# Delaying the first store of a DMA-streamed SiLU-multiply by one small DVE copy, so that it is not issued together with a load

## The chip, the cores, the metric

One core of one Trainium2 chip. The metric is the device time of one execution in microseconds (us), the median of a few runs. The profiler's span of one execution (from the program's first to its last instruction) is about 1.8 us shorter than that time, and is used only to compare spans with spans.

DVE is the vector engine, ACT the scalar engine, SP the sync engine, which only issues DMAs here. A load or a store is one DMA: an engine issues it into its queue, 16 DMA engines move it, and it lands when all of it has arrived. The trace records it in packets; a packet here is the piece that one DMA engine moves at a time, one contiguous run of one partition.

## The reference

```python
def setup_inputs():
    batch, seq, dim = (32, 512, 2048)
    return {'x': np.random.randn(batch, seq, dim).astype(np.float32)}

def reference(x):
    half_dim = x.shape[-1] // 2
    x1, x2 = x[..., :half_dim], x[..., half_dim:]          # (copies cut)
    silu_x1 = x1 * (1 / (1 + np.exp(-x1)))
    return (silu_x1 * x2).astype(np.float32)
```

134.22 MB are read and 67.11 MB written, with two light elementwise operations between them.

## The kernel before

The 16384 rows are cut into 16 tiles; a tile has 128 partitions with 8 rows each. Two input buffers (64 KB per partition each) and two output buffers (32 KB each) are used in turn. Loads are issued from ACT's queue, stores from SP's. After the multiplies of tile i, the store of tile i and the load of tile i+2 are both released by the same event, the last multiply.

```python
    K = 8
    KC = 2
    # ... (cut: tile plan, pools with bufs=2 each, views)
    def load(i):
        xt = in_pool.tile([P, K, in_cols], dt, name="xt")
        nc.scalar.dma_start(out=xt[:, :plan[i][1], :], in_=view(x_flat, i))
        loaded[i] = xt

    load(0)
    load(1)
    for i in range(n_tiles):
        # ... (cut)
        for c in range(0, k, KC):
            ce = min(c + KC, k)
            nc.scalar.activation(out=ot[:, c:ce, :], in_=xt[:, c:ce, :half], func=Silu)
            nc.vector.tensor_mul(out=ot[:, c:ce, :], in0=ot[:, c:ce, :], in1=xt[:, c:ce, half:])
            if last:
                nc.sync.dma_start(out=ov[:, c:ce, :], in_=ot[:, c:ce, :])
        if not last:
            nc.sync.dma_start(out=ov, in_=ot[:, :k, :])
        if i + 2 < n_tiles:
            load(i + 2)
```

## Time and profile before

| quantity | before | where it is read |
|---|---|---|
| time, median | 470.84 us (470.56 to 471.13, 3 runs) | the runs |
| span of the profiled run | 468.9 us | page |
| bytes moved, mean rate | 201.35 MB, 429 GB/s | page |
| DVE and ACT busy | 30%, 25% | page |
| DMA in a tile period of 29 us | share 1.00, 432 to 434 GB/s | table by windows |

The page of the kernel before, its lines on engines and DMA. A digit in the DMA line is the busy share of one fortieth of the span, in tenths; 9 means 90% or more.

```profile
span 468.9 us, 269 instructions
DVE 142.3 (30%) x64; ACT 118.2 (25%) x65; POOL 0.2 (0%) x4
DMA  9899999999999998999999999999999989999998
DMA packets 5042, 201.35 MB, mean 429 GB/s; under 512 B 560, under 2 KB 560, under 8 KB 560
```

No compute engine is busy for even a third of the time, while the DMA line stands at 8 or 9 in every slice. The table by windows of the same kernel says it more sharply. Its columns are the stretch, its length, each engine's busy time with the number of instructions, the clock, the share of the 16 DMA engines' time that was busy, and what they moved. (A share a little over 1 comes of counting each packet where it starts.)

```profile
core 0: us, DVE busy (x) ACT busy (x) POOL busy (x), PEclk, DMA share, GB/s
44.50:73.50 29.00, 8.89 (x4) 7.31 (x4) 0.00 (x0) 1.00 1.00 434
73.50:102.50 29.00, 8.90 (x4) 7.31 (x4) 0.00 (x0) 1.00 1.00 434
422.00:451.00 29.00, 8.89 (x4) 7.31 (x4) 0.00 (x0) 1.00 1.00 432
451.00:467.00 16.00, 8.90 (x4) 7.31 (x4) 0.00 (x0) 1.00 0.99 421
```

Even the end, from 451 us on, after the last load has landed, is full of stores. The timeline around the first store (start, duration, engine, line, operation; in brackets the idle time before and what ended it; an "x3" merges three issues into one line):

```profile
21.88 7.31 ACT L87 ACTIVATE ot<-xt 128x2048 f32<-128x2048 f32 x4 [19.31 <-DMA xt<-in_x_dram]
23.82 8.90 DVE L92 TENSOR_TENSOR ot<-ot,xt 128x2048 f32<-128x2048 f32 x4 [23.82 <-ACT ot L87]
32.74 51.99 SPq L100 DMA_DIRECT2D out_dram<-ot  x3
32.75 0.35 ACTq L74 DMA_DIRECT2D xt<-in_x_dram  x1
44.54 7.31 ACT L87 ACTIVATE ot<-xt 128x2048 f32<-128x2048 f32 x4 [15.36 <-DMA xt<-in_x_dram]
46.48 8.89 DVE L92 TENSOR_TENSOR ot<-ot,xt 128x2048 f32<-128x2048 f32 x4 [13.77 <-ACT ot L87]
55.41 0.37 ACTq L74 DMA_DIRECT2D xt<-in_x_dram  x1
73.53 7.31 ACT L87 ACTIVATE ot<-xt 128x2048 f32<-128x2048 f32 x4 [21.68 <-DMA xt<-in_x_dram]
```

The first store and load 2 are issued 5 ns apart. Load 1 lands at 44.5 us, 11.8 us after load 2 was issued; load 3 is issued at 55.4 us, and load 2 lands at 73.5. So the load queue always holds work. The chain of waits (start, duration, what) alternates between a load and 8.91 us of multiplies:

```profile
55.41 47.19 DMA xt<-in_x_dram
102.60 0.02 issue
102.62 1.92 ACT ot L87
104.54 0.02 issue
104.57 8.91 DVE ot L92 x4
113.47 0.02 issue
113.50 47.07 DMA xt<-in_x_dram
```

### The profile page before, as it was taken

To read this page: it belongs to the slowest core of one execution; us is meant where nothing else is said; L and a number is where in the kernel's file an instruction comes from. 1 tells how busy PE (TensorE), PEld (TensorE's weight loads), DVE (VectorE), ACT (ScalarE), POOL (GpSimd) and SP (SyncE) were. 2 spreads that over 40 slices of the span, in tenths; PEclk is the share of its full clock that TensorE was granted. 3 is DMA by queue.
4 is the path that set the end of the run, shared out by engine and by line. 5 is a ranking of instruction groups with operands and counts; after the bars stand their busy time and mean duration, and the time that the engine had idled before them with its cause. 6 is when DMAs were issued, how large, how long until landed. Compare 5 with 4: busy or idle time off the path is not lost.

```text
span 468.9 us, 269 instructions
## 1 busy us (share of the span) xinstructions
DVE 142.3 (30%) x64; ACT 118.2 (25%) x65; POOL 0.2 (0%) x4
## 2 busy tenths in 40 slices
DVE  0070705106061160601507025070250702407034
ACT  1142406023060330603206032060420604106051
POOL 0000000000000000000000000000000000000000
DMA  9899999999999998999999999999999989999998
GB/s 431 375 447 403 447 447 447 403 419 431 447 447 403 447 492 363 442 492 391 458 403 439 456 447 403 409 442 447 447 403 444 467 386 447 442 419 481 400 409 354
DMA packets 5042, 201.35 MB, mean 429 GB/s; under 512 B 560, under 2 KB 560, under 8 KB 560
## 3 DMA queue, kind: packets, MB, share of 16 engines
q10 hardware_dynamic: 2304, 134.22, 66.4%
q1 hardware_dynamic: 2736, 67.11, 33.2%
q14 instruction: 2, 0.02, 0.0%
HBM read 134.22 MB, written 67.11 MB: 429 GB/s over the span
## 4 chain that ended last, share of the span: by engine, by line
DMA 80%; DVE 15%; ACT 3%; DVEq 0%; issue 0%
DMA xt<-in_x_dram 80%; DVE ot L92 15%; ACT ot L87 3%; DVEq L128 0%
## 5 line engine op out<-in xcount | busy, mean ns | idle before, releaser
L92 DVE TENSOR_TENSOR ot<-ot,xt 128x2048 f32<-128x2048 f32 x64 | 142.3, 2286 | 319.5 <-ACT ot L87 319.5
L87 ACT ACTIVATE ot<-xt 128x2048 f32<-128x2048 f32 x64 | 116.9, 1897 | 338.8 <-DMA xt<-in_x_dram 338.8
L87 ACT ACT_TABLE_LOAD x1 | 1.3, 1283 | 1.3 <-PEq L117 1.3
L117 POOL MEMSET const-uint8-127<- 128x1 uint8 x1 | 0.1, 102 | 0.0
L117 POOL MEMSET const-bfloat16-1.0<- 128x1 bf16 x1 | 0.1, 101 | 0.0
L117 POOL MEMSET const-float32-0.0<- 128x1 f32 x1 | 0.1, 98 | 0.2 <-issue 0.2
L117 POOL MEMSET const-float32-1.0<- 128x1 f32 x1 | 0.1, 98 | 0.0
## 6 DMA issues: line engine op xcount, KB each, us to landing
out_dram<-ot SPq DMA_DIRECT2D x15, 4096.0 KB, 39.8
out_dram<-ot SPq DMA_DIRECT2D x4, 1024.0 KB, 5.7
xt<-in_x_dram ACTq DMA_DIRECT2D x16, 47.1
```

Source lines behind the costliest of these rows:

```text
L87: nc.scalar.activation(out=ot[:, c:ce, :], in_=xt[:, c:ce, :half], func=mybir.ActivationFunctionType.Silu,)
L92: nc.vector.tensor_mul(out=ot[:, c:ce, :], in0=ot[:, c:ce, :], in1=xt[:, c:ce, half:],)
L117: nc = _bacc.Bacc("TRN2", target_bir_lowering=False, num_devices=1)
```

## The change

The intent is that the first store should not be issued at the same moment as load 2. The store must wait for a copy that rewrites one row of its tile; the load waits for the multiplies only.

```diff
                 nc.sync.dma_start(out=ov[:, c:ce, :], in_=ot[:, c:ce, :])
+        if i == 0:
+            nc.vector.tensor_copy(out=ot[:, k - 1, :], in_=ot[:, k - 1, :])
         if not last:
             nc.sync.dma_start(out=ov, in_=ot[:, :k, :])
```

## The prediction

> **What bounds the kernel now.** The 16 DMA engines, all the time. The page gives 201.35 MB at a mean of 429 GB/s over a span of 468.9 us; DVE is busy 30%, ACT 25%. The table by windows shows a DMA share of 1.00 and 432 to 434 GB/s in every 29 us tile period. In the trace's packets a 64 KB load packet takes 2.42 us and a 32 KB store packet 1.21 us on an engine; all packets of an engine make about 465 us, of a window from 1.1 to 467 us. Load and store packets alternate, and no queue empties after the first store: each load is issued 11.8 us before the previous one lands (chain of waits, timeline), each store about 11 us before the previous one lands. DVE's 8.91 us per tile is on the drawn chain but hides behind those queued transfers. The Trainium skill ("DMA: Bandwidth & Descriptors", section "Issuing engines are not separate DMA queues") says that both issuing engines share the same 16 DMA engines and interleave; this trace agrees.
>
> **What the change does.** It removes nothing. It adds one DVE copy of 128x1024 f32, after tile 0 only. The multiply of 128x2048 takes 2.286 us, so at its rate the copy takes an estimated 1.2 us; the skill ("VectorE: DVE Perf Modes", section "Mode 2×_2P") gives f32 copies twice the rate, about 0.7 us. No instruction of this trace shows which. DVE idles 13.8 us there, so tile 1 isn't touched. The first store's issue moves from 32.75 us to about 33.5 us (34.0 at the slow rate). Load 2 stays at 32.75 us. Later pairs are still issued together.
>
> **How much lies on the critical path.** Almost nothing. Meanwhile the engines have load 1 (until about 43 us) and then load 2. The first store's packets, now at 38.9 us, stay or move by one load packet (2.42 us), and loads move ahead by the same work. The store of tile 0 lands at 66.2 us, 7.3 us before load 2 at 73.5 us, so its buffer is still free in time. At the end one more store packet may be queued behind the last load, so the tail stays full. Bytes and packet sizes are the same.
>
> The only loss that the change could remove: load packets that start at 35.7 us, just before the first store's, take 3.2 to 3.4 us in place of 2.42 on all 16 engines, 0.8 us lost once. Later pairs, also issued within 5 ns, show none, so I take it for the cost of the store queue's first use, which stays. If it came from the simultaneous issue it would go: 0.8 us (0.2%).
>
> **Prediction: 470.7 us, 469.4 to 472.0.** Faster by over 2%: 0.01; within 2%: 0.97; slower by over 2%: 0.02. A gain of 2% (9 us) is not there: only 2 to 4 us of the span are not moving packets.
>
> **What would show it.** A DVE copy of 0.6 to 1.2 us after tile 0's multiplies; the first store issued that much after load 2; the long packets near 35.7 us still there, or gone for 0.8 us; tile periods of 29.0 us, DMA share 1.00; the last load within 3 us of 451.0 us, the end within 1 us of 468.9.
>
> **What would make it wrong.** If the shifted order of packets lowered the rate in all tile periods: 0.6 us a tile would be 2%. If the later store made tile 2's activation wait for its buffer until the load queue ran empty, which needs a delay over 11 us. If load 2 waited for the copy, that would only cost hidden issue time.

## The result, and the profile after

| | before | after |
|---|---|---|
| time, median | 470.96 us (470.56 to 471.13, 4 runs) | 470.93 us (470.67 to 471.56, 4 runs) |
| ratio | | 1.0002, 95% interval 0.9985 to 1.002 |
| span of the profiled run | 468.9 us | 468.9 us |
| first store issued | 32.74 us | 33.53 us |
| its first packet | 38.88 us | 38.86 us |
| last load landed | 451.00 us | 451.03 us |

Ratios, here and below, are the mean time of one kernel's runs over that of the other's of the same rounds, so not quite the ratio of the medians quoted. Executions over 1.5% slower than the fastest of the same kernel are left out of the means.

The page of the kernel after:

```profile
span 468.9 us, 270 instructions
DVE 143.0 (31%) x65; ACT 118.2 (25%) x65; POOL 0.2 (0%) x4
DMA  9899999999999998999999999999999989999998
DMA packets 5042, 201.35 MB, mean 429 GB/s; under 512 B 560, under 2 KB 560, under 8 KB 560
L101 DVE COPY ot<-ot 128x1024 f32<-128x1024 f32 x1 | 0.7, 695 | 0.0
```

One instruction more, 0.695 us of DVE; the DMA line is the same digit for digit. The table by windows of the kernel after:

```profile
44.50:73.50 29.00, 8.90 (x4) 7.31 (x4) 0.00 (x0) 1.00 1.00 434
73.50:102.50 29.00, 8.90 (x4) 7.31 (x4) 0.00 (x0) 1.00 1.00 434
422.00:451.00 29.00, 8.89 (x4) 7.31 (x4) 0.00 (x0) 1.00 1.00 432
451.00:467.00 16.00, 8.90 (x4) 7.31 (x4) 0.00 (x0) 1.00 0.99 421
```

The timeline after, around the first store:

```profile
23.88 8.90 DVE L92 TENSOR_TENSOR ot<-ot,xt 128x2048 f32<-128x2048 f32 x4 [23.88 <-ACT ot L87]
32.81 0.33 ACTq L74 DMA_DIRECT2D xt<-in_x_dram  x1
32.81 0.69 DVE L101 COPY ot<-ot 128x1024 f32<-128x1024 f32 x1
33.53 51.22 SPq L103 DMA_DIRECT2D out_dram<-ot  x3
44.71 7.31 ACT L87 ACTIVATE ot<-xt 128x2048 f32<-128x2048 f32 x4 [15.47 <-DMA xt<-in_x_dram]
46.65 8.90 DVE L92 TENSOR_TENSOR ot<-ot,xt 128x2048 f32<-128x2048 f32 x4 [13.15 <-ACT ot L87]
```

The chain of waits after, the same stretch:

```profile
55.59 47.02 DMA xt<-in_x_dram
102.60 0.02 issue
102.63 1.92 ACT ot L87
104.55 0.02 issue
104.57 8.91 DVE ot L92 x4
113.48 0.02 issue
113.50 47.12 DMA xt<-in_x_dram
```

The load issued at 55.59 us in place of 55.41 lands at the same 102.60 us: what is issued later just waits less.

The change did to the issues just what it was meant to: the store now follows the load by 0.72 us. Nothing followed from it. On the DMA engines the first store packet starts when it did before, because those engines were busy with packets of load 1. On idle engines a store's first packet starts 0.9 us after its issue (delay27 below), so before about 33.6 us and after about 34.4 us. Each engine was then on a load packet that ran until about 35.7 us, and it took one more load packet before the store's. (Why one more, the records don't show; in delay4 and every_store_later it is up to two.) The copy used up 0.8 us of a wait that was 6.1 us long before (32.74 to 38.88) and 5.3 us long after (33.53 to 38.86). From there on the packets follow one another as before: the n-th load or store packet of the one trace starts within 0.25 us of that of the other, to the end. On an engine it reads as follows, L for a 64 KB load packet and S for a 32 KB store packet (my reading of the packet records, the first two tile periods):

```
before  L L L L L L L L L L L L L L L* S L S S L S L S L S L S L S L L S L S S L S L ...
after   L L L L L L L L L L L L L L L* S L S S L S L S L S L S L S L L S L S S L S L ...
        an L takes 2.418 us, an S 1.213 us; L* takes 3.2 to 3.4 us in both
```

All packets of one engine at these durations make 465.0 us; the window from the first packet to the last is 466.5 us. So about 1.5 us in the whole program are lost in packets that take too long: 0.6 us in the very first packets, and 0.8 to 0.9 us in L*, the last load packet before the first store packet. L* is the only thing that the change could have removed, and it is still there.

The Trainium skill ("DMA: Bandwidth & Descriptors", section "Queues, rings and completion order") says that each DMA engine takes turns between the queues that have work, a packet at a time. The trace agrees: L and S alternate, one to one, wherever both queues hold work. Since a load has 8 packets of 64 KB per engine and tile and a store 8 of 32 KB, one-to-one turns use up both at the same pace. The two places in a period where two S or two L follow each other are where the turn of the other queue goes to the four-byte record that signals a completion. The section "Where 436 GB/s comes from" puts the ceiling of the fabric at 435 GB/s; the trace shows 434 in a period. There is no room for a gain of even 2%.

### The profile page after: what moved, and what is told of

The parts are those of the page before. It is cut to its first block, busy times and chain, and to the rows that moved or that the text cites. A ratio compares the mean times of both kernels' runs of the same rounds, so it can differ in the third digit from the quotient of the medians.

```text
span 468.9 us, 270 instructions
## 1 busy us (share of the span) xinstructions
DVE 143.0 (31%) x65; ACT 118.2 (25%) x65; POOL 0.2 (0%) x4
## 4 chain that ended last, share of the span: by engine, by line
DMA 80%; DVE 15%; ACT 3%; DVEq 0%; issue 0%
DMA xt<-in_x_dram 80%; DVE ot L92 15%; ACT ot L87 3%; DVEq L131 0%
## 5 line engine op out<-in xcount | busy, mean ns | idle before, releaser
L92 DVE TENSOR_TENSOR ot<-ot,xt 128x2048 f32<-128x2048 f32 x64 | 142.3, 2286 | 318.8 <-ACT ot L87 318.8
```

## The experiments

Theory A: the DMA engines always have packets, so a delay of a DMA's issue costs or gains nothing as long as another queue holds work. Rival B: load 2 and the first store collide, which is what L* is, and a better separation would gain 0.8 us. Rival C: the separation gains something and the delay by the copy eats it. Part of my prediction was also that L* is the price of the store queue's first use; D, E and F below are its rivals. Twelve kernels ran. "Before" in each table is the kernel before, run on the same chip between them.

### A longer delay of the first store: 4.4, 26.7 and 40.1 us

```diff
         if i == 0:
-            nc.vector.tensor_copy(out=ot[:, k - 1, :], in_=ot[:, k - 1, :])
+            for _ in range(N):          # delay4: N = 1, delay27: N = 6, delay40: N = 9
+                nc.vector.tensor_copy(out=ot[:, :k, :], in_=ot[:, :k, :])
```

delay4:

> In place of one row, the whole of tile 0 is copied in place, so the first store is issued about 4.4 us after load 2[...]. Theory A (the DMA engines are never without packets, and the long load packets before the first store are the price of the store queue's first use): same time within 0.3%; the first store's packets come one or two load packets (2.42 or 4.84 us) later than 38.9 us; the long packets move with them, one or two places later, and stay 0.6 to 1.0 us too long. Rival B (the long packets come of issuing load 2 and the first store together, or of load 2's issue): they stay at 35.7 us, or are gone, for 0.8 us (0.2%) less. Rival C (a gain by the separation is cancelled by the delay of the copy): about 3.7 us slower (0.8%) with the longer delay.

delay27:

> The whole of tile 0 is copied six times, so the first store is issued about 26.5 us after tile 0's multiplies, and tile 1's multiplies wait for DVE too. Theory A, by stepping the packets of one engine through with the durations of the trace: load 1 and load 2 keep the engines busy to about 59 us without any store, the loss is 0.5 us, 471.5 us in all; the end of the program has the same packets queued. Rival C: 26 us slower (5.5%). My prediction on record said that harm needs a delay over 11 us; if A holds with this run even 26 us are free.

delay40:

> Nine copies, about 39.8 us. Theory A: load 2 is done at about 59 us, the first store comes at about 73 us and load 3, which waits for tile 1's multiplies, not before; so the engines stand idle for about 14 us and the time rises by just that, to about 485 us (+3%). Rival C: about 39 us slower (+8%).

| run | store held back by | time, median | before | ratio, 95% interval |
|---|---|---|---|---|
| delay4 | 4.4 us | 470.66 us | 471.45 us | 0.9985 (0.9973 to 0.9998) |
| delay27 | 26.7 us | 472.39 us | 471.45 us | 1.0024 (1.0009 to 1.004) |
| delay40 | 40.1 us | 485.69 us | 471.45 us | 1.0307 (1.0293 to 1.0321) |

Rival C falls: a delay of 26.7 us, some 38 times as long as the change's copy, cost about 1 us. The table by windows of delay27 and of delay40 shows where the loss begins. First delay27:

```profile
33.00:59.00 26.00, 25.83 (x6) 7.31 (x4) 0.00 (x0) 1.00 1.02 444
59.00:73.00 14.00, 9.33 (x6) 2.05 (x2) 0.00 (x0) 1.00 1.08 412
```

Then delay40:

```profile
33.00:59.00 26.00, 25.79 (x7) 7.31 (x4) 0.00 (x0) 1.00 1.02 444
59.00:73.00 14.00, 13.90 (x4) 0.00 (x0) 0.00 (x0) 1.00 0.00 0
```

Up to 59 us the engines run at the full rate on loads 1 and 2 alone, without any store. Then there is nothing left to load, because load 3 needs the buffer of tile 1, whose multiplies stand behind the copies on DVE. In delay27 the store arrives at that very moment (issued at 59.44 us), in delay40 at 73.28 us: 14.0 us with a DMA share of 0.00, and a time that is 14.2 us longer. The delay itself is free; what costs in delay40 is a time in which both queues are empty. The prediction said that harm needs a delay of over 11 us. That is not wrong, but the number was not the limit: for this way of delaying, the real one lies near 26 us. The copies hold back tile 1's multiplies as well, and with them load 3; a store held back alone for so long was not run.

delay27 lost its time in another way. Two lines of its timeline (the "x3" merges three store issues):

```profile
59.44 22.70 SPq L104 DMA_DIRECT2D out_dram<-ot  x3
68.25 0.37 ACTq L74 DMA_DIRECT2D xt<-in_x_dram  x1
```

By the packet records its engines idled only about 0.4 us, at 60 us. The first store then ran alone, and no packet was long before it or in it. When load 3 started beside it at 70 us, one store and one load packet of each engine took 1.7 us too long together (1.8 us in delay40, at 84 us); L* at 35.7 us was gone. This bears on what L* is, below.

delay4 also answers rival B. The store was issued 4.5 us after the load, and its first packet came 4.6 us later than in the kernel before (43.46 us). The long packets moved with it, from 35.7 to 40.3 us, two packets later, and summed up to 0.64 us per engine against 0.87 before. They belong to the store's arrival, not to the simultaneous issue. The ratio of delay4 lies 0.15% under 1 with an interval that only just excludes 1; the kernel before itself ran between 470.69 and 471.92 us on that chip, and the profiled spans are 468.9 us for both. I don't call it a gain.

### Every store held back, not only the first

```diff
-        if i == 0:
-            nc.vector.tensor_copy(out=ot[:, k - 1, :], in_=ot[:, k - 1, :])
+        if not last:
+            nc.vector.tensor_copy(out=ot[:, :k, :], in_=ot[:, :k, :])
```

> The copy of the whole tile (about 4.4 us of DVE) stands before the store of every tile but the last, so that no pair of load and store is issued at one time. Theory A: same within 0.3%, although DVE is busy about 66 us more. Rival B' (each simultaneous issue costs something small at each tile): faster, by up to 15 times the cost. Rival C: up to 4.4 us a tile slower, 60 us in all.

Measured: 470.72 us against 471.45 before, ratio 0.9988 (0.9974 to 1.0001): the same. Two lines of the page of this run, then two of its timeline:

```profile
span 469.1 us, 270 instructions
DVE 208.8 (45%) x79; ACT 118.2 (25%) x65; POOL 0.2 (0%) x4
```

```profile
52.15 4.43 DVE L101 COPY ot<-ot 128x8192 f32<-128x8192 f32 x1
71.59 7.31 ACT L87 ACTIVATE ot<-xt 128x2048 f32<-128x2048 f32 x4 [23.01 <-DMA out_dram<-ot]
```

DVE does 66.5 us of extra work (208.8 against 142.3) for nothing in time. Even the reason for the waits has changed: tile 2's activation now waits for the store that frees its output buffer, where it waited for its load before. The chain of waits is drawn through stores in this run, and the span is the same to 0.2 us. With the engines full, it doesn't matter which transfer the chain goes through. A separation of all 15 pairs also gains nothing: rival B falls at the later tiles, too.

### The mirror: load 2 held back in place of the first store

```diff
         if not last:
             nc.sync.dma_start(out=ov, in_=ot[:, :k, :])
+        if i == 0:
+            nc.vector.tensor_copy(out=xt[:, k - 1, half:], in_=xt[:, k - 1, half:])
```

(an edit of the kernel before, without the change)

> The mirror of the change: the copy of one row is of tile 0's input, after its multiplies, so load 2 follows it by about 0.7 us and the first store goes at once. Theory A: same within 0.3%, order of packets as before, long packets at 35.7 us as before. Rival B: the long packets are gone or moved.

Measured: 471.33 us against 471.04 before, ratio 1.0001 (0.9987 to 1.0014). Load 2 was issued 0.79 us after the store; the order of packets was that of before, and the long packets were at 35.6 us, 3.30 to 3.56 us long. Rival B falls again.

### Fewer bytes

```diff
-            nc.sync.dma_start(out=ov, in_=ot[:, :k, :])
+            nc.sync.dma_start(out=ov[:, :k - 1, :], in_=ot[:, :k - 1, :])
```

(in the changed kernel; the result is wrong, one row in eight of tiles 0 to 14 is never written)

> The changed kernel, but tiles 0 to 14 store seven rows of eight (a wrong result on purpose): 7.86 MB less of 201. Theory A: the time falls by what those 120 packets of 32 KB cost, 15 x 1.21 us on each engine = 18.2 us, less a few us at the end where the engines run out of stores before the last tile's are ready: by stepping the packets through, 15.8 us, to about 455 us (-3.4%). A kernel bound by the chain of compute and waits instead would stay at 471 us.

Measured: 452.86 us against 471.04, ratio 0.961 (0.9597 to 0.9623). The store packets took 1.062 us in place of 1.213, so 120 of them save 18.1 us on an engine, and 18.2 us is what the medians differ by. My estimate of 15.8 us allowed too much for idle time at the end. The rate in the steady part did not change, as one line of the table by windows shows:

```profile
51.00:430.00 379.00, 120.11 (x55) 95.94 (x53) 0.00 (x0) 1.00 1.00 435
```

This is the experiment that shows what binds: taking bytes away pays in full, where 66 us of DVE work cost nothing. Whether the DMA engines themselves, the way to the memory or the memory sets the length of a packet, no run here separates.

### Load and store both held back, at every tile but the last

```diff
         if not last:
+            for _ in range(N):          # both9: N = 2, both18: N = 4
+                nc.vector.tensor_copy(out=xt[:, :k, half:], in_=xt[:, :k, half:])
+                nc.vector.tensor_copy(out=ot[:, k - 1, :2], in_=ot[:, k - 1, :2])
             nc.sync.dma_start(out=ov, in_=ot[:, :k, :])
```

(in the kernel before)

> The kernel before, with two copies of the whole second half of the input tile (and of two columns of the output, to hold the store) after the multiplies of each tile but the last: load i+2 and store i are still issued together, but about 8.9 us later, under the 11.8 us by which each load is issued ahead of the previous one's landing. Theory A, by stepping packets through: +2 us at most (473 us). Bound by the chain: +8.9 us a tile in half of the steps of the chain, some 65 us more.

> The same with four copies, about 17.7 us, which is more than the 11.8 us ahead: the load queue must run empty before each load. Theory A: it costs, but much less than the excess suggests, as stores fill some of it: by stepping the packets through about +19 us (490 us, +4%), with the DMA share under 1.00 in each tile period. If the 11.8 us were not the slack that I take it for, the time would be either unchanged or up by over 60 us.

| run | time, median | before | ratio, 95% interval |
|---|---|---|---|
| both9 | 474.11 us (473.97 to 476.23) | 471.10 us | 1.0063 (1.0046 to 1.0079) |
| both18 | 509.82 us (505.75 to 511.88) | 471.10 us | 1.0811 (1.0759 to 1.0863) |

A delay of 8.9 us in every tile cost 3 us in all at the median. The profiled run was the slowest of the four (476.23 us, its span 5.6 us over that of before). It lost most of this at the two ends: 2.5 us without packets between 20 and 44 us, where load 1 was through before load 2 was issued, and 2.2 us more idle time than before after 451 us. Stretched packets made 0.6 us more than before. From 102 to 451 us both9 runs at full rate. The table by windows, both9 first:

```profile
102.00:451.00 349.00, 214.33 (x96) 87.71 (x48) 0.00 (x0) 1.00 1.00 434
```

Then both18:

```profile
51.00:480.00 429.00, 368.18 (x165) 102.32 (x56) 0.00 (x0) 1.00 0.98 403
```

both9 confirms that the multiplies, and whatever stands between them and the next issue, have slack. My figure of 11.8 us for it, in the prediction and in these expectations, was wrong for all tiles but the first: it is how far load 2 is issued ahead of load 1's landing, and from load 3 on it is 18.1 us, as the timeline of before shows. A delay of 17.7 us (both18) leaves 0.4 us of that, less than the 0.9 us that a DMA takes from its issue to its first packet on idle engines (delay27), so the load queue can run empty. both18 cost 38.7 us and not the 19 us that I had worked out by stepping the packets through. The packet records say why. An engine stood idle for 20.3 us more than in the kernel before, which is what stepping the packets through had given (about 19 us); 11.3 of them fall between 33 and 59 us, before load 2 and the first store start. The other half was not in my model: the packets themselves took 22.4 us more than their usual durations, against 1.5 us before. Both together are 41.2 us, and the two profiled spans, 510.1 and 468.9 us, differ by 41.2 us. The DMA share of 0.98 hides this, since a stretched packet counts as busy; the 403 GB/s beside it does not. The stretches are 1.2 to 1.6 us in each tile period. Most of each lies where the next load and the next store, issued within 20 ns of each other, start just as the last packets of the previous pair end: both queues have run empty together, and in most periods the first packet of each is long. I take them for the same kind of thing as L*, and they come back.

### What L* is: the store queue used early, and a small store early

```diff
     load(1)
+    warm = out_pool.tile([P, K, half], dt, name="ot")
+    nc.sync.dma_start(out=warm[:, 0, :64], in_=view(x_flat, 0)[:, 0, :64])
```

(warm_load, in the kernel before)

> The kernel before, with one small load (128 rows of 256 bytes, overwritten later) issued at the start on the queue that the stores use, so that this queue has been used before the first store. If the long load packets before the first store are the price of the queue's first use, as I predicted: they are gone at 35.7 us (2.42 us each), the time falls by 0.8 us less what the small load costs, so 0 to 0.8 us faster (within 0.2%). Rival D (they are the price of the first write to HBM, whatever the queue had done): still 0.6 to 1.0 us too long, the time unchanged or some tenths of a us longer.

```diff
+            if i == 0 and c == 0:
+                nc.sync.dma_start(out=ov[:, c:ce, :], in_=ot[:, c:ce, :])
             if last:
                 # ... (cut)
+        if i == 0:
+            nc.sync.dma_start(out=ov[:, KC:, :], in_=ot[:, KC:k, :])
-        if not last:
+        elif not last:
             nc.sync.dma_start(out=ov, in_=ot[:, :k, :])
```

(early_store, in the kernel before)

> The kernel before, with the first quarter of tile 0 stored right after its first multiply (about 26 us) and the other three quarters after the last. The first issue on the store queue is then 6.6 us away from any load's. First-use or first-write price: long packets of 0.6 to 1.0 us extra, just before the first store packets at about 31 us, none at 35.7 us. Rival B (they come of the simultaneous issue with load 2): none near 31 us, and still near 35.7 us. Time within 0.3% in both.

warm_load took 471.67 us against 471.04, ratio 1.001 (0.9997 to 1.0024); early_store 470.62 us against 471.04, ratio 0.9987 (0.9974 to 1.0001). The long packets, collected from the packet records of all runs in which they were looked for (a packet counts if it took over 0.2 us too long):

```
run                first store  its first    long load packets   their          sum per
                   issued, us   packet, us   start at, us        duration, us   engine, us
before             32.74        38.88        35.7 to 36.0        3.18 to 3.42   0.87
after              33.53        38.86        35.5 to 36.1        3.15 to 3.34   0.82
load2_later        33.09        39.00        35.6 to 36.4        3.30 to 3.56   1.00
warm_load          33.10        39.14        35.8 to 36.4        3.17 to 3.50   0.92
delay4             37.30        43.46        40.3 to 41.0        2.64 to 3.36   0.64
every_store_later  37.29        43.94        40.4 to 40.9        3.38 to 3.62   1.05
early_store        26.30        30.76        39.4 to 39.8        2.62 to 2.84   0.27
```

In warm_load the store queue had finished a small load at 24.6 us, 8.5 us before the first store, and L* came as before. So L* is not the price of the queue's first use, and that step of my prediction is wrong. (The small load itself, in packets of 256 bytes from 6.7 to 21.9 us beside load 0 and load 1, stretched none of theirs.) In early_store neither expectation came true: the load packets before the first store packets (8 KB each there, from 30.8 us) took the usual 2.42 us, none was long at 35.7 us, and a smaller stretch came at 39.4 us. So the stretch does not follow whenever a store comes first, and its size is not fixed; small packets seem to cause less of it, which I have not tested by itself. In delay27 and delay40, not in the table, the first store started in an engine's idle time and nothing was stretched; the stretch came when load 3 started beside it. So it belongs to one queue starting while the other is at work, and it can be the load's start as well as the store's. Whether the start itself counts, or the change from reads alone (or writes alone) to reads and writes mixed, no run here separates.

### Does L* come back when the store queue runs empty in every tile?

```diff
-        nc.scalar.dma_start(out=xt[:, :plan[i][1], :], in_=view(x_flat, i))
+        for h in (0, K // 2):
+            nc.scalar.dma_start(out=xt[:, h:h + K // 2, :],
+                                in_=view(x_flat, i)[:, h:h + K // 2, :])
```

(split_load, in the kernel before)

> The kernel before, with each load issued as two loads of four rows each (32 KB packets, 16 per engine and tile in place of 8 of 64 KB); same bytes, right result. Packets of the two queues alternate one to one, so the store of a tile (8 packets) is through when half of the load's 16 packets are, and the store queue runs empty for about 9.7 us in each tile period, while the load queue never does. Theory E (each time a queue that has run empty starts again beside a busy one, 0.6 to 1.1 us are lost, which is what the long packets at 35.7 us are): a stretch in each tile period, 15 x 0.4 to 1.1 us, so 6 to 16 us slower (1.3 to 3.4%). Theory F (the long packets are paid once, at the first write to HBM in the program): one stretch, 471 to 472 us, within 0.3%.

```diff
         if not last:
-            nc.sync.dma_start(out=ov, in_=ot[:, :k, :])
+            nc.sync.dma_start(out=ov[:P // 2], in_=ot[:P // 2, :k, :])
```

(half_store, in the kernel before, wrong result)

> The kernel before, but tiles 0 to 14 store only partitions 0 to 63 (a wrong result on purpose): 4 store packets of 32 KB per engine and tile beside 8 load packets of 64 KB, so the store queue is empty for about 10 us of each tile period, the load queue never. Packets alone: 128 x 2.418 + 60 x 1.213 + 9.9 = 392.2 us, with the ends about 397 us. Theory E: 15 stretches of 0.4 to 1.1 us in the load packets, one per tile, so 403 to 413 us. Theory F: one stretch, 397 to 400 us.

split_load ran from 481.73 to 507.50 us; only the run of 481.73 us counts as fast, the other five, the profiled one among them, as slow. No ratio can be given, and I draw nothing from its profile. That its fastest run is 10.6 us (2.2%) over the median of before is what theory E expected (6 to 16 us), but one run is not a verdict.

half_store took 416.77 us at the median (413.04 to 423.24, one of four slow), against 471.15 before, ratio 0.8819 (0.8778 to 0.886). Theory F, a price paid once at the first write, expected 397 to 400 us. Theory E expected 403 to 413 us, and the time is over that, too. In the profiled run (413.04 us) the packets of an engine took 9.4 us too long in all (the small ones of the last tile left out), of which 0.6 us are the start, 1.0 us the packets at 35.6 us, and the rest is spread over the later tile periods with 0.2 to 0.9 us in most of them. By these records theory F falls: long packets come back, 0.6 us a tile on average ((9.4 - 0.6)/15). But they don't follow each restart of the store queue. Around the 14 restarts after the first they make 0 to 0.9 us, six times 0.13 us or less, and 4.5 us together of the 7.8 us that are lost after the first; so theory E is right in part at most. A further 6.8 us (408.9 us from the first to the last packet, less 402.1 us of packets) are idle time, nearly all between 391 and 400 us, where the loads have run out and the last tile's stores aren't ready; theory E did not have it. That long packets can come when a queue starts anew beside a busy one is shown by delay27 and delay40 (a load's start), and that they can come many times by both18; how they arise in the engines, and what sets their size, is open.

## Why the prediction was right, point by point

- **What bounds the kernel**: right. 434 GB/s and a DMA share of 1.00 in the tile periods before and after; fewer bytes paid in full (seven_rows: 18.2 us measured, 18.1 us of packets), more DVE work cost nothing (every_store_later: 66.5 us for no change).
- **The copy**: right, 0.695 us, near the estimate of 0.7 us made from the skill's page on DVE modes. The 128x8192 copies took 4.43 us; between the two sizes an element of a partition costs 0.52 ns ((4.43 - 0.695)/7168), against 1.12 ns in the multiply (2.286/2048). The trace agrees with a doubled rate for f32 copies ("VectorE: DVE Perf Modes", section "Mode 2×_2P").
- **The first store moves, load 2 doesn't, tile 1 isn't touched**: right (33.53 us, load 2 at 32.81 us). The first store packet did not move at all.
- **Its buffer is still free in time**: right and not even needed. In delay4 and every_store_later the activation of tile 2 did wait for the store, without a loss.
- **Time and range**: 470.7 us (469.4 to 472.0) against 470.93 us measured.
- **"I take it for the cost of the store queue's first use, which stays"**: half right. It stays, as predicted, and it does not come from the simultaneous issue (delay4, load2_later, every_store_later). But it is not the queue's first use: warm_load used the queue before, and L* stayed (0.92 us). The first use of the store queue beside no load had no long packets (delay27), and long packets come again when queues that have run empty start again (both18; in half_store not at each start). The number predicted did not depend on which it was.
- **"each load is issued 11.8 us before the previous one lands"**: wrong but for the first of them; 18.1 us from load 3 on. The error was on the safe side.
- **"which needs a delay over 11 us"**: a safe bound, but not the limit. A one-time delay of 26.7 us cost 1 us. The wait that the prediction named, tile 2's activation waiting for its output buffer, came already at 4.4 us (delay4) and cost nothing; in delay27 the load queue ran empty because the copies held back load 3.

## What to carry to other kernels

When the DMA engines are busy at their full rate and every queue has work waiting, the moment at which a DMA is issued is not the moment at which it runs; shifting an issue by less than the work that is queued ahead changes nothing, and neither does removing compute from the drawn chain of waits. Before moving an issue, count what the engines have in hand at that time, and look for times when all queues are empty: only bytes and such times can be won. No version with a right result is clearly faster than both kernels. Keep the queues from running empty, since in both18 each restart cost 1.2 to 1.6 us in packets that took longer (in half_store 0.6 us a tile on average, not all of it at restarts), which a busy share does not show.

## What the Trainium skill lacked or had wrong

- "DMA: Bandwidth & Descriptors", section "Where 436 GB/s comes from", says that for transfers between HBM and SBUF the HBM side, about 358 GB/s per core, binds. Here one core alone moved 434 GB/s of reads and writes in each tile period, near the 435 GB/s that it gives for the fabric. The page's own note under "Measured" that its numbers hold with the other core idle fits this better.
- The same page, section "Latency and other measured facts", gives about 600 ns to the first byte of such a DMA. With idle engines the trace shows 0.86 and 0.88 us from the start of the first store's issue to its first packet (delay40, delay27), and 1.0 us for the first load. The issuing instruction itself takes 0.37 us in delay40, so from its end it is 0.5 us; the section doesn't say from where it counts. Beside a busy queue it was 4.5 to 6.7 us (early_store, every_store_later), which that section doesn't mention: the new queue's first packet waits while an engine ends its load packet and takes one or two more, 2.42 us each.
- No page tells of the stretch of packets that can come when a queue starts from empty: 0.6 to 1.1 us once in most runs here, 0.3 us in early_store, 1.7 and 1.8 us once in delay27 and delay40, 1.2 to 1.6 us a tile in both18, about 0.6 us a tile on average in half_store.
- The same page, section "SWDGE vs HWDGE vs iDMA", has a packet at 4096 bytes preferably, as the point where an engine changes queues, in its table on what GpSimd builds. The DMAs here are issued from ACT and SP, so the row may not be meant for them. In the records turns change after 64 KB of a load and 32 KB of a store, each one contiguous run per partition. That made the two queues drain at one pace here, by the tile's shape; the page doesn't say that the length of a contiguous run sets the share that each queue gets.
